# The mLSTM over x in two chunks of 256 tokens with a second state between them, in place of one chunk of 512

## The chip, the cores and the metric

The kernel runs on one core of a Trainium2 chip. Its time is the device time of one execution in microseconds. TensorE (PE, with its weight loads as PEld), VectorE (DVE), ScalarE (ACT), GpSimd (POOL) and the queues of SyncE (SP) that issue DMAs each work through a list of instructions of their own in order, and wait for one another by semaphores. Matmul operands and results of the vector engines lie in SBUF, matmul results in PSUM.

## The reference

Two layers run over 512 tokens `x` and 256 context tokens `ctx`. In each, the tokens are normalised and projected (`w_in`), go through three mixers side by side (an mLSTM of 4 heads of 128, a Fourier mix, a convolution of 31 taps), are projected back (`w_out`) and go through an MLP of 4096. The second layer gives out x alone, so its context goes only through what the mLSTM needs of it. The mLSTM is a linear attention with gates, run forward and backward. The reference goes chunk by chunk (64 tokens) and carries a state `C`, `n`, `m`:

```python
def step(carry, inp):
    C, n, m = carry
    ...
    S = jnp.einsum('bhld,bhsd->bhls', qc, kc) * jnp.exp(D - m_t[..., None])
    num = w_inter[..., None] * jnp.einsum('bhed,bhld->bhle', C, qc) + jnp.einsum('bhls,bhse->bhle', S, vc)
    den = w_inter * jnp.einsum('bhd,bhld->bhl', n, qc) + jnp.sum(S, axis=-1)
    h = num / jnp.maximum(jnp.abs(den), jnp.exp(-m_t))[..., None]
    ...
    C_new = decay[..., None, None] * C + jnp.einsum('bhs,bhse,bhsd->bhed', ws, vc, kc)
    n_new = decay[..., None] * n + jnp.einsum('bhs,bhsd->bhd', ws, kc)
```

The context goes first and its last state is the first state of x, in both directions. The length of a chunk changes only the order of the sums: inside a chunk every pair of tokens is a score, across chunks the state stands for what came before.

## The kernel before

**Tiles.** All 768 tokens (256 of the context, 512 of x, in blocks of 128) stay in SBUF. The large products take each operand as a rounded part and a remainder (`hi`, `lo`; L219 and L220 make them for the weights, L230 and L233 for the activations) and three matmuls in place of one. Weights come by DMA in the order of `stream`, two pieces ahead (`prep`, L213).

**Order.** A tile framework lays out the program: it takes the instructions in the order of the code, with priorities, and fixes for each engine the list in which they run. The taps of the convolution (L679, DVE) have a lower priority, so they fill DVE's gaps. A pool of tiles hands its buffers out in the order of the code: `t4` has 8 buffers of 4 KB per partition, `c2` 5 of 2 KB, `aux` and `mm` 4 PSUM banks each. `tc.cur_priority` and the pools are all that sets the order here.

**The mixer of a layer.** The chunks of `w_in` are taken in the order `CHUNKS`: t, a, t, a, then q, k, o for each of the four heads, then the Fourier chunk. `stationary` (L463) is the product of one chunk: 24 weights by 512 tokens of x, with the context 24 more by 256. After the o chunk of head h the generator `mlstm(h)` is staged, and each later chunk advances it by a step, so the work of a head lies between the products of the next head's chunks. Its three steps, for x:

- step 1: the split of q and k (L230, L233), the broadcast of the row of maxima `mb` by DMA (L814), for the state of the context two transposes of k (L818), their four weightings `kw` on ACT (L822) and four matmuls (L842, 129 columns: 128 of v and one of ones) into `cp`, copied to `cs` (L844). `qs` is q times the weight of the state (L825 on ACT, L826 on DVE). For each of the four key blocks j of x the scores against all 512 queries (L793, three matmuls of 512 columns), the weights exp (L836, ACT) over the 512, 384, 256 or 128 queries that each direction needs, the triangle of the diagonal block cut out on POOL (`masked`, L771), and the product of weights and scores (L838, DVE) into the tile `E`.
- step 2: for each query block and direction the sum in PSUM of the state's term and of one term for each key block (L862; 28 matmuls of 129 columns for x), then the quotient and the moments on DVE (`head_out`, L748 to L760).
- step 3: the transposes back (L777) and the gate (`group_out`).

The context, in the first layer only, has a step 1 and 2 of its own with one chunk of 256 (L793, L804, L807), which the change does not alter in what it computes. On POOL's queue, beside the masks, stand the DMAs of the Fourier tables (L196), which wait for a weight buffer. `gate_columns` makes the small columns of weights (`pcol`, `em`, `wc`); the row of maxima goes through HBM (`md`, L637) and comes back as `m0` (L647).

Of the kernel before, what the change touches and what calls it, by code (L numbers as in the profile page):

```python
# [10 lines left out]
F32 = mybir.dt.float32  # L11
F32R = mybir.dt.float32r
AF = mybir.ActivationFunctionType
ALU = mybir.AluOpType
# [3 lines left out]
SEQ = 512  # L18
CTX = 256
TOK = CTX + SEQ  # L20
NB = TOK // 128
CB = CTX // 128
# [26 lines left out]
ZW = 2 * 1 + 1 + TOK  # L49
QW = ZW - 2  # L50
XQ = CTX + 1
PAD = 15

DEFER, TAPS, LATER, AHEAD, PER = 1, 7, 300, 2, 3
# [10 lines left out]
def build(tc, a):  # L65
# [6 lines left out]
    small = pool("small", 2)  # L72
# [13 lines left out]
    def nm(s):  # L86
        n_names[0] += 1
        return f"{s}{n_names[0]}"

    def t4(*dims):  # L90
        t = t4p.tile([128, 1024], F32, tag="t4", name=nm("t4_"))
        return t
# [4 lines left out]
    def c2():  # L97
        return c2p.tile([128, 512], F32, tag="c2", name=nm("c2_"))
# [4 lines left out]
    def aux():  # L103
        return aup.tile([128, 512], F32, tag="aux", name=nm("aux_"))
# [4 lines left out]
    V, S, P, T = nc.vector, nc.scalar, nc.gpsimd, nc.tensor  # L109
    dma = nc.sync.dma_start  # L110
# [31 lines left out]
    ident = cload("ident", [128, 128])  # L142
# [8 lines left out]
    md = [drp.tile([8, TOK], F32, name=f"md{l}") for l in range(DEPTH)]  # L151
# [322 lines left out]
    def layer(l, res, nbg, first=None):  # L474
# [22 lines left out]
        vt = [t3()[:, :NB * 129].rearrange("p (b n) -> p b n", b=NB) for _ in range(H)]  # L497
# [111 lines left out]
        for q in range(2):  # L609
            ps = aux()  # L610
            for i in range(3):
# [3 lines left out]
                         bias=cols[64:128, C_BG:C_BG + 1])  # L615
# [24 lines left out]
        pcol = small.tile([128, NB, 2, 4], F32, tag="pcol", name=nm("pcol"))  # L640
        em = small.tile([128, NB, 2, 4], F32, tag="em", name=nm("em"))
        wc = small.tile([128, CB, 2, 4], F32, tag="wc", name=nm("wc"))
        mdv = md[l][:].rearrange("(d h) t -> h d t", d=2)

        m0 = small.tile([128, 2, 4], F32, tag="m0", name=nm("m0"))
        for d, t0 in ((0, CTX - 1), (1, 0)):
            dma(m0[:, d, :], md[l][4 * d:4 * d + 4, t0].partition_broadcast(128))  # L647

        def gate_columns():
            for q in range(2):  # L650
                ps = aux()
                for i in range(3):
                    T.transpose(ps[:, 128 * i:128 * i + 128], pm[:, 128 * (3 * q + i):128 * (3 * q + i) + 128], ident)
                v4 = ps[:, :384].rearrange("p (b g d n) -> p b g d n", b=3, g=2, d=2)
                for i in range(3):
                    V.tensor_copy(pcol[:, 3 * q + i], v4[:, i, 0, :, 0:4])
                    S.activation(em[:, 3 * q + i], v4[:, i, 1, :, 0:4], AF.Exp, scale=-1.0)
            for j in range(CB):
                V.tensor_tensor(wc[:, j], pcol[:, j], m0, ALU.subtract)
            S.activation(wc, wc, AF.Exp)  # L660

        y = {}

# [59 lines left out]
        def short_conv(outs, w, ranges):  # L723
# [12 lines left out]
            if i0 == 0:  # L736
                P.memset(q[:, CTX:XQ], 0.0)
            for k in (0, 2):
                V.scalar_tensor_tensor(q[:, i0:QW], zq[:, i0 + k:QW + k], w(k), q[:, i0:QW], ALU.mult, ALU.add)
            return q  # L740

        def kcol(j):
            return 128 * j if j < CB else XQ + 128 * (j - CB)

        def head_out(ps, b, h, hn, ba):
            den = ps[:, 128:258:129]
            d = ty(2, "d")
# [21 lines left out]

        def masked(E, fwd):  # L770
            P.affine_select(E, E, pattern=[[1 if fwd else -1, 128]], compare_op=ALU.is_ge, fill=0.0, base=0,  # L771
                            channel_multiplier=-1 if fwd else 1)
# [10 lines left out]
        def mlstm(h, q, k, to):  # L783
            y[h] = t3()
            groups = []
            qh, ql, kh, kl = [t3(F32R) for _ in range(4)]
            i0 = XQ if last else 0
            for src, hi, lo in ((q, qh, ql), (k, kh, kl)):
                split(src[:, i0:QW], hi[:, i0:QW], lo[:, i0:QW], True)

            def scores(out, kc, q0, n):
                for i, (kp_, qp) in enumerate(((kh, qh), (kh, ql), (kl, qh))):
                    T.matmul(out, kp_[:, kc:kc + 128], qp[:, q0:q0 + n], start=i == 0, stop=i == 2)  # L793

            if not last:
                mb = c2().rearrange("p (d t) -> p d t", d=2)
                dma(mb, mdv[h, :, 0:CTX].partition_broadcast(128))
                qk = aux()
                E = t4().rearrange("p (j d t) -> p j d t", j=2, d=2)
                for j in range(2):  # L800
                    scores(qk[:, 256 * j:256 * j + 256], 128 * j, 0, CTX)
                for j, d in ((0, 0), (0, 1), (1, 0), (1, 1)):
                    lo, hi = (128 * j, CTX) if d == 0 else (0, 128 * j + 128)
                    S.activation(E[:, j, d, lo:hi], mb[:, d, lo:hi], AF.Exp, scale=-1.0,  # L804
                                 bias=pcol[:, j, d, h:h + 1])
                    masked(E[:, j, d, 128 * j:128 * j + 128], d == 0)
                    V.tensor_tensor(E[:, j, d, lo:hi], E[:, j, d, lo:hi], qk[:, 256 * j + lo:256 * j + hi], ALU.mult)  # L807

                def c_terms(b, d, E=E):
                    js = range(0, b + 1) if d == 0 else range(b, CB)  # L810
                    return [(E[:, j, d, 128 * b:128 * b + 128], vt[h][:, j, :]) for j in js]
                groups.append((0, range(CB), c_terms))
            mb = t4().rearrange("p (d t) -> p d t", d=2)
            dma(mb, mdv[h, :, CTX:TOK].partition_broadcast(128))  # L814

            kp = aux()
            for j in range(CB):
                T.transpose(kp[:, 128 * j:128 * j + 128], k[:, 128 * j:128 * j + 128], ident)  # L818
            kw = c2().rearrange("p (d j n) -> p d j n", d=2, j=CB)
            for d in range(2):  # L820
                for j in range(CB):
                    S.activation(kw[:, d, j, :], kp[:, 128 * j:128 * j + 128], AF.Copy, scale=wc[:, j, d, h:h + 1])  # L822
            qs = t4().rearrange("p (d t) -> p d t", d=2)
            for d in range(2):
                S.activation(qs[:, d, :], mb[:, d, :], AF.Exp, scale=-1.0, bias=m0[:, d, h:h + 1])  # L825
            V.tensor_tensor(qs, qs, q[:, XQ:XQ + SEQ].unsqueeze(1).to_broadcast([128, 2, SEQ]), ALU.mult)  # L826
            Es = {}
            for j in range(CB, NB):
                qk = aux()
                scores(qk, kcol(j), XQ, SEQ)  # L830
                E = t4().rearrange("p (d t) -> p d t", d=2)
                Es[j] = E
                s0 = 128 * (j - CB)
                for d in range(2):
                    lo, hi = (s0, SEQ) if d == 0 else (0, s0 + 128)
                    S.activation(E[:, d, lo:hi], mb[:, d, lo:hi], AF.Exp, scale=-1.0, bias=pcol[:, j, d, h:h + 1])  # L836
                    masked(E[:, d, s0:s0 + 128], d == 0)
                    V.tensor_tensor(E[:, d, lo:hi], E[:, d, lo:hi], qk[:, lo:hi], ALU.mult)  # L838
            cp = aux()
            for d in range(2):  # L840
                for j in range(CB):
                    T.matmul(cp[:, 129 * d:129 * d + 129], kw[:, d, j, :], vt[h][:, j, :], start=j == 0, stop=j == CB - 1)  # L842
            cs = c2()[:, :258]
            S.activation(cs, cp[:, :258], AF.Copy)  # L844

            def x_terms(b, d):
                s0 = 128 * (b - CB)
                js = range(CB, b + 1) if d == 0 else range(b, NB)
                return [(qs[:, d, s0:s0 + 128], cs[:, 129 * d:129 * d + 129])] + \
                       [(Es[j][:, d, s0:s0 + 128], vt[h][:, j, :]) for j in js]  # L850
            groups.append((CTX, range(CB, NB), x_terms))
            yield
            hns = []
            for t0, bs, terms in groups:
                hn = c2()
                ba = tiny.tile([128, 4, 2], F32, tag="ba", name=nm("ba"))
                for i, b in enumerate(bs):
                    ps = aux()
                    for d in range(2):
                        ts = terms(b, d)  # L860
                        for n, (st_, mv) in enumerate(ts):
                            T.matmul(ps[:, 129 * d:129 * d + 129], st_, mv, start=n == 0, stop=n == len(ts) - 1)  # L862
                    head_out(ps, b, h, hn[:, 128 * i:128 * i + 128], ba[:, i])
                r = rsd(ba, len(bs))
                for i in range(len(bs)):
                    hb = hn[:, 128 * i:128 * i + 128]
                    V.tensor_scalar(hb, hb, ba[:, i, 0:1], r[:, i:i + 1], ALU.subtract, ALU.mult)
                hns.append((hn, 128 * len(bs), t0))
            yield
            for hn, n, t0 in hns:  # L870
                group_out(hn, n, t0, h, to)
# [583 lines left out]
```

## Time and profile before

| | |
|---|---|
| median of 3 runs | 1532.19 us (1530.03 to 1533.87) |
| profiled execution, its own time | 1534.91 us |
| its span | 1532.9 us |
| TensorE busy | 1488.5 us, 97% |
| DVE, ACT, POOL busy | 1101.4, 754.9, 94.0 us |
| granted TensorE clock | 0.998 |

Busy time is a sum over the span. TensorE's busy share says that it is rarely idle, not how fast it is; a stretch of the timeline tells how far apart its matmuls start. The mixer of the first layer with its mLSTM lies at about 140 to 340 us, that of the second at 960 to 1140. The trace records an fp32 matmul (L842, L862) twice and a transpose or an fp32r matmul (L818, L793) once.

### The profile page before, as it was taken

What the parts mean: (1) busy time and instruction counts of PE and PEld (TensorE: products, weight loads), DVE (VectorE), ACT (ScalarE), POOL (GpSimd) and SP (SyncE); (2) the same over time, 40 slices, a digit from 0 to 9 for tenths busy, and PEclk for the clock granted to TensorE, in tenths of its full rate; (3) what the DMA queues carried; (4) which work ended last, traced back from release to release, by engine and by line L of the source; (5) the groups of instructions that cost most, each with busy time, mean ns of one, the idle gap of its engine ahead of it and who ended that gap; (6) DMA issues with size and microseconds to landing.
All of it is one profiled execution on the core that took longest, in us unless ns stands there. A gap on an engine that the chain in (4) does not pass through costs nothing. (4 is left out here: it accounts for less than half of the span.)

```text
span 1532.9 us, 23301 instructions
## 1 busy us (share of the span) xinstructions
PE 1488.5 (97%) x8926; PEld 1303.6 (85%) x8926; DVE 1101.4 (72%) x2129; ACT 754.9 (49%) x1471; POOL 94.0 (6%) x233
## 2 busy tenths in 40 slices
PE   7999999999999999999999999999999999999998
PEld 4878888887888898898988979877888889999887
DVE  3359997754899886666865575898756886677666
ACT  4634245535745352442534576544437665555544
POOL 0002012200100000000000010111101000000000
PEclk9999999999999999999999999999999999999999
DMA  8445435523532452442622343422224133332224
GB/s 330 140 159 186 158 125 194 199 83 117 186 124 92 146 189 76 158 132 88 193 86 80 99 171 105 129 78 78 88 71 166 66 111 110 111 109 91 83 94 148
DMA packets 66015, 197.30 MB, mean 129 GB/s; under 512 B 11952, under 2 KB 14416, under 8 KB 65904
## 3 DMA queue, kind: packets, MB, share of 16 engines
q1 hardware_dynamic: 64464, 191.10, 37.5%
q0 software_dynamic: 1440, 4.72, 1.0%
q8 instruction: 70, 1.15, 0.3%
q14 instruction: 41, 0.34, 0.1%
HBM read 183.13 MB, written 12.66 MB: 128 GB/s over the span
## 5 line engine op out<-in xcount | busy, mean ns | idle before, releaser
L219 ACT ACTIVATE hi<-raw 128x1024 fp32r<-128x1024 f32 (+1 forms) x245 | 244.1, 999 | 397.0 <-PE mm L1052 134.9
L1052 PE MATMUL mm<-hi,t 128*128 128x512 f32 (+1 forms) x1296 | 406.1, 391 | 0.0
L220 DVE TENSOR_TENSOR lo<-raw,hi 128x1024 fp32r<-128x1024 f32 (+1 forms) x245 | 280.7, 1148 | 75.4 <-ACT hi L219 37.6
L1052 PEld LDWEIGHTS mm<-hi,t 128*128 128x128 f32 x1296 | 242.4, 188 | 54.7 <-DVE t L1220 0.4
L1052 PE MATMUL mm<-lo,t 128*128 128x512 f32 (+1 forms) x648 | 253.7, 391 | 0.0
L463 PE MATMUL mm<-hhi,hi 128*128 128x256 f32 (+1 forms) x576 | 168.3, 336 | 0.0
L463 PE MATMUL mm<-hlo,hi 128*128 128x256 f32 (+1 forms) x576 | 166.0, 332 | 0.0
L463 PE MATMUL mm<-hhi,lo 128*128 128x256 f32 (+1 forms) x576 | 165.0, 331 | 0.0
L1052 PEld LDWEIGHTS mm<-lo,t 128*128 128x128 f32 x648 | 121.8, 188 | 26.0
L1121 PE MATMUL mm<-hhi,hi 128*128 128x384 f32 (+1 forms) x448 | 139.5, 311 | 3.0 <-ACT c L1147 1.8
L1121 PE MATMUL mm<-hhi,lo 128*128 128x384 f32 (+1 forms) x448 | 138.5, 309 | 1.5 <-DVE lo L220 1.5
L1220 DVE TENSOR_TENSOR t<-mm,t 128x512 f32<-128x512 f32 x120 | 81.8, 688 | 79.5 <-PE mm L1052 79.4
L1121 PE MATMUL mm<-hlo,hi 128*128 128x384 f32 (+1 forms) x448 | 138.4, 309 | 0.0
L463 PEld LDWEIGHTS mm<-hhi,hi 128*128 128x128 f32 x576 | 107.1, 188 | 15.0 <-issue 2.5
L463 PEld LDWEIGHTS mm<-hhi,lo 128*128 128x128 f32 x576 | 108.3, 188 | 11.0
L463 PEld LDWEIGHTS mm<-hlo,hi 128*128 128x128 f32 x576 | 108.0, 188 | 11.0 <-issue 0.4
L679 DVE SCALAR_TENSOR_TENSOR t<-t,half,t 128x783 f32<-128x783 f32 (+1 forms) x120 | 102.3, 889 | 0.4
L1121 PE MATMUL mm<-t,hi 128*128 128x384 f32 (+1 forms) x448 | 97.4, 308 | 0.0
L1121 PEld LDWEIGHTS mm<-hhi,hi 128*128 128x128 f32 x448 | 84.4, 188 | 6.8 <-ACT c L1147 3.0
L1121 PEld LDWEIGHTS mm<-hhi,lo 128*128 128x128 f32 x448 | 84.3, 188 | 1.9 <-DVE lo L220 1.9
L1121 PEld LDWEIGHTS mm<-hlo,hi 128*128 128x128 f32 x448 | 84.4, 188 | 1.2
L233 DVE TENSOR_TENSOR t<-c,t 128x256 fp32r<-128x256 f32 (+1 forms) x132 | 62.2, 478 | 31.9 <-ACT t L230 31.5
(245 smaller groups left out, 2732.2 us busy)
## 6 DMA issues: line engine op xcount, KB each, us to landing
raw<-w SPq DMA_DIRECT2D x128, 512.0 KB, 4.3
raw<-w_at SPq DMA_DIRECT2D x48, 512.0 KB, 3.6
raw<-w_a SPq DMA_DIRECT2D x44, 512.0 KB, 4.3
raw<-w_c SPq DMA_DIRECT2D x32, 512.0 KB, 3.5
xd<-t SPq DMA_DIRECT2D x20, 512.0 KB, 2.9
raw<-w_o SPq DMA_DIRECT2D x16, 512.0 KB, 6.0
t<-xd SPq DMA_DIRECT2D x20, 256.0 KB, 6.0
t<-x SPq DMA_DIRECT2D x8, 512.0 KB, 6.0
```

What stands on the lines that cost most here:

```text
L219: S.activation(hi[:, r0:n0], raw[:, r0:n0], AF.Copy)
L220: V.tensor_tensor(lo[:, r0:n0], raw[:, r0:n0], hi[:, r0:n0].bitcast(F32), ALU.subtract)
L233: V.tensor_tensor(blk_lo, src, blk_hi.bitcast(F32), ALU.subtract)
L463: T.matmul(o[:, :n], wp[:, k, :], hp[:, k, t0:t0 + n], start=k == 0 and i == 0, stop=k == KB - 1 and i == 2)
L679: V.scalar_tensor_tensor(o, u[j][:, o0 + k:o1 + k], w, o, ALU.mult, ALU.add)
L1052: T.matmul(ps, hp[:, 128 * b:128 * b + 128], wp[:, f % 2, c0:c1], start=f == fs[0] and at[0] == 0 and n == 0, stop=f == fs[-1] and at[1] = ...
L1121: T.matmul(ps[:, :HN], wp[:, K2 * j + k, :], hp, start=first and k == 0 and i == 0, stop=k == K2 - 1 and i == 2, skip_group_check=True)
L1220: V.tensor_tensor(ac_, ps, ac_, ALU.add)
```

## The change

x is taken in two chunks of 256 (`CH`). Scores and weights are made inside a chunk alone (`weighted`, which the context now uses as well), so each chunk has two key blocks by 256 queries. Between the chunks stands a second state `cs1` for each direction: k of the chunk that comes first in that direction is transposed (L841: four transposes) and weighted (`kx`, L843, four on ACT), multiplied with v (L862, four matmuls), and the first state, decayed by `dec`, is added on DVE (L866). The second chunk's queries take `cs1` in place of `cs`. The exponent of `qs` is now four activations of 256 columns. `m1`, the maxima at the border, comes by two more small DMAs; `wx` and `dec` are made in `gate_columns`. `kw` and `kx` now lie in one tile of `t4`, where `kw` had one of `c2`.

```diff
+            for i in range(4):
+                V.tensor_tensor(wx[:, i], pcol[:, CB + i, i // 2], m1[:, i // 2], ALU.subtract)
+            S.activation(wx, wx, AF.Exp)
+            V.tensor_tensor(dec, m0, m1, ALU.subtract)
+            S.activation(dec, dec, AF.Exp)
...
+            def weighted(mb, kc, q0, blk):
+
+                qk = aux()
+                E = t4().rearrange("p (j d t) -> p j d t", j=2, d=2)
+                for j in range(2):
+                    scores(qk[:, CH * j:CH * j + CH], kc + 128 * j, q0, CH)
+                for j, d in ((0, 0), (0, 1), (1, 0), (1, 1)):
+                    lo, hi = (128 * j, CH) if d == 0 else (0, 128 * j + 128)
+                    S.activation(E[:, j, d, lo:hi], mb[:, d, lo:hi], AF.Exp, scale=-1.0,
+                                 bias=pcol[:, blk + j, d, h:h + 1])
+                    masked(E[:, j, d, 128 * j:128 * j + 128], d == 0)
+                    V.tensor_tensor(E[:, j, d, lo:hi], E[:, j, d, lo:hi], qk[:, CH * j + lo:CH * j + hi], ALU.mult)
+                return E
...
+            kt = t4()
+            kw = kt[:, 0:512].rearrange("p (d j n) -> p d j n", d=2, j=CB)
+            kx = kt[:, 512:1024].rearrange("p (i n) -> p i n", i=4)
...
-            kw = c2().rearrange("p (d j n) -> p d j n", d=2, j=CB)
...
+            kp = aux()
+            for i in range(4):
+                T.transpose(kp[:, 128 * i:128 * i + 128], k[:, XQ + 128 * i:XQ + 128 * i + 128], ident)
+            for i in range(4):
+                S.activation(kx[:, i, :], kp[:, 128 * i:128 * i + 128], AF.Copy, scale=wx[:, i, h:h + 1])
             qs = t4().rearrange("p (d t) -> p d t", d=2)
             for d in range(2):
-                S.activation(qs[:, d, :], mb[:, d, :], AF.Exp, scale=-1.0, bias=m0[:, d, h:h + 1])
+                for c in range(2):
+                    m_ = m0 if c == d else m1
+                    S.activation(qs[:, d, CH * c:CH * c + CH], mb[:, d, CH * c:CH * c + CH], AF.Exp, scale=-1.0,
+                                 bias=m_[:, d, h:h + 1])
...
-            for j in range(CB, NB):
-                qk = aux()
-                scores(qk, kcol(j), XQ, SEQ)
-                E = t4().rearrange("p (d t) -> p d t", d=2)
...
+            Ex = [weighted(mb[:, :, CH * c:CH * c + CH], XQ + CH * c, XQ + CH * c, CB + 2 * c) for c in range(2)]
...
+            cp = aux()
+            for d in range(2):
+                for j in range(2):
+                    i = 2 * d + j
+                    T.matmul(cp[:, 129 * d:129 * d + 129], kx[:, i, :], vt[h][:, CB + i, :], start=j == 0, stop=j == 1)
+            cs1 = c2()[:, :258]
+            for d in range(2):
+                dd = slice(129 * d, 129 * d + 129)
+                V.scalar_tensor_tensor(cs1[:, dd], cs[:, dd], dec[:, d, h:h + 1], cp[:, dd], ALU.mult, ALU.add)
...
-                js = range(CB, b + 1) if d == 0 else range(b, NB)
-                return [(qs[:, d, s0:s0 + 128], cs[:, 129 * d:129 * d + 129])] + \
-                       [(Es[j][:, d, s0:s0 + 128], vt[h][:, j, :]) for j in js]
+                c = (b - CB) // 2
+                return [(qs[:, d, s0:s0 + 128], (cs if c == d else cs1)[:, 129 * d:129 * d + 129])] + \
+                    within(Ex[c], b, CB + 2 * c, d)
```

On TensorE, step 1 of the second layer's first head stands before as follows (`t_1617` and `t_1619` are the split q and k, `aux` the PSUM banks, `c_1623` is `kw`; of the twelve scores the first of two banks and the last of all are shown):

```order
L818 MATMUL aux_9736<-ident_sb,t_1606_9641 128x128 x2
L793 MATMUL aux_9748<-t_1617_9726,t_1619_9728 128x512
...
L793 MATMUL aux_9759<-t_1617_9726,t_1619_9728 128x512
...
L793 MATMUL aux_9781<-t_1617_9726,t_1620_9729 128x512
L842 MATMUL aux_9792<-t_1516_8895,c_1623_9739 128x129 x4
L463 MATMUL mm_9821<-hhi,hi_9654 128x256
```

With the change the same place reads (lines are those of the changed kernel; `t_1624` holds `kw` and `kx`; of the twelve scores the first and the last):

```order
L835 MATMUL aux_9789<-ident_sb,t_1608_9693 128x128 x2
L841 MATMUL aux_9796<-ident_sb,t_1608_9693 128x128 x4
L801 MATMUL aux_9811<-t_1619_9778,t_1621_9780 128x256
...
L801 MATMUL aux_9831<-t_1619_9778,t_1622_9781 128x256
L855 MATMUL aux_9851<-t_1515_8935,t_1624_9788 128x129 x4
L862 MATMUL aux_9858<-t_1515_8935,t_1624_9788 128x129 x4
L464 MATMUL mm_9888<-hhi,hi_9706 128x256
```

Four banks of scores became two, four transposes and four matmuls of the second state were added, and the state's bank comes third and fourth after the two banks of the transposes.

On ACT, in the second layer, the weights of the second head (tile `t_1679` is its `mb`) stand before in this order, the last of its eight ahead of its own `kw` (L822):

```order
L825 ACTIVATE t_1682_10069<-t_1679_10059,m_9359 128x512 x2
L836 ACTIVATE t_1684_10077<-t_1679_10059,pcol_9356 128x512
L836 ACTIVATE t_1684_10077<-t_1679_10059,pcol_9356 128x128
...
L836 ACTIVATE t_1686_10088<-t_1679_10059,pcol_9356 128x384
...
L836 ACTIVATE t_1690_10110<-t_1679_10059,pcol_9356 128x512
...
L822 ACTIVATE c_1681_10064<-aux_10061,wc_9358 128x128 x4
```

With the change (`t_1680` is `mb`, `t_1681` holds `kw` and `kx`) the second head's work on ACT is one row of instructions:

```order
L838 ACTIVATE t_1681_10120<-aux_10121,wc_9398 128x128 x4
L843 ACTIVATE t_1681_10120<-aux_10128,wx_9402 128x128 x4
L848 ACTIVATE t_1684_10137<-t_1680_10118,m_9399 128x256
...
L811 ACTIVATE t_1686_10144<-t_1680_10118,pcol_9396 128x256
...
L811 ACTIVATE t_1688_10164<-t_1680_10118,pcol_9396 128x256
L857 ACTIVATE c_1690_10188<-aux_10183 128x258
```

The weights of the state and all the exponents of x moved behind the transposes of the same head's k.

## Rows read from the trace of the kernel before

**Rows 1.** The page, part 1: busy us (share of the span), instructions
```profile
PE 1488.5 (97%) x8926; PEld 1303.6 (85%) x8926; DVE 1101.4 (72%) x2129; ACT 754.9 (49%) x1471; POOL 94.0 (6%) x233
```

**Rows 2.** Busy us by stretch: length, PE, PEld, DVE, ACT, POOL, clock, DMA share, GB/s
```profile
140.00:240.00 100.00, 99.06 (x695) 81.47 (x697) 90.91 (x198) 33.53 (x65) 11.57 (x33) 1.00 0.43 144
240.00:340.00 100.00, 97.68 (x649) 87.38 (x650) 71.25 (x209) 49.23 (x104) 19.68 (x44) 1.00 0.52 172
960.00:1060.00 100.00, 95.61 (x505) 79.83 (x505) 91.33 (x159) 48.52 (x89) 12.33 (x37) 1.00 0.29 93
1060.00:1140.00 80.00, 78.29 (x487) 68.58 (x486) 59.45 (x172) 34.45 (x67) 12.35 (x29) 1.00 0.27 88
```

**Rows 3.** Waits of TensorE, 140 to 340: us in total, times, longest
```profile
PE aux L777 <- DVE c L867: 2.6, 2, 1.7
```

**Rows 4.** Waits of TensorE, 960 to 1140
```profile
PE aux L777 <- DVE c L867: 2.3, 2, 1.4
PE aux L793 <- DVE t L233: 1.6, 2, 0.8
PE aux L842 <- DVE t L838: 1.3, 1, 1.3
```

**Rows 5.** Timeline of TensorE: start us, us, engine, line, form, count
```profile
159.77 0.87 PE L793 MATMUL aux<-t,t 128*128 128x256 f32 x6
160.48 0.38 PE L818 MATMUL aux<-ident_sb,t 128*128 128x128 f32 x2
...
1086.02 3.11 PE L793 MATMUL aux<-t,t 128*128 128x512 f32 x12
1088.97 1.05 PE L842 MATMUL aux<-t,c 128*128 128x129 f32 x8
...
1118.71 0.38 PE L862 MATMUL aux<-c,t 128*128 128x129 f32 x2
...
1124.73 0.39 PE L862 MATMUL aux<-t,t 128*128 128x129 f32 x2
1124.88 0.48 PE L903 MATMUL aux<-hi,t 128*128 128x512 f32 x1
...
1190.96 1.09 PE L423 MATMUL aux<-ident_sb,t 128*128 128x128 f32 x8 [0.64 <-ACT t L410]
```

**Rows 6.** Groups by line and form: busy us, mean ns | idle before
```profile
L771 POOL TENSOR_SCALAR_AFFINE_SELECT t<-t 128x128 f32<-128x128 f32 x80 | 41.3, 537 | 226.3 <-ACT t L836 147.5 <-ACT em L657 67.5 <-ACT t L804 10.2
...
L753 DVE SCALAR_TENSOR_TENSOR c<-aux,rd,c 128x128 f32<-128x128 f32 x40 | 13.8, 345 | 0.0
...
L838 DVE TENSOR_TENSOR t<-t,aux 128x256 f32<-128x256 f32 x16 | 6.0, 414 | 0.0
...
L838 DVE TENSOR_TENSOR t<-t,aux 128x128 f32<-128x128 f32 x16 | 4.5, 280 | 0.0
```

**Rows 7.** Timeline of ScalarE, second layer's first head
```profile
990.42 2.50 ACT L836 ACTIVATE t<-t,pcol 128x128 f32<-128x128 f32 x6
...
1009.28 1.13 ACT L822 ACTIVATE c<-aux,wc 128x128 f32<-128x128 f32 x4
```

**Rows 8.** Timeline of VectorE, the products of that head
```profile
1014.02 3.27 DVE L838 TENSOR_TENSOR t<-t,aux 128x512 f32<-128x512 f32 x8
```

**Rows 9.** The chain, 1005 to 1025: start us, us, what
```profile
1014.02 0.89 DVE t L838 x2
...
1014.95 1.16 PE aux L842 x8
1016.11 8.32 PE mm L463 x48
```

**Rows 10.** Waits of all engines
```profile
POOL lo L196 <- PE mm L463: 15.1, 2, 11.2
```

**Rows 11.** Timeline of the SyncE queue
```profile
978.99 0.97 SPq L647 DMA_DIRECT2D m<-md  x2
```

More of the change, by code (lines that the diff above doesn't have):

```diff
@@ L51 @@
 XQ = CTX + 1
+CH = 256
 PAD = 15
@@ L645, in layer @@
         m0 = small.tile([128, 2, 4], F32, tag="m0", name=nm("m0"))
-        for d, t0 in ((0, CTX - 1), (1, 0)):
+        m1 = small.tile([128, 2, 4], F32, tag="m1", name=nm("m1"))
+        dec = small.tile([128, 2, 4], F32, tag="dec", name=nm("dec"))
+        wx = small.tile([128, 4, 4], F32, tag="wx", name=nm("wx"))
+        for d, t0, t1 in ((0, CTX - 1, CTX + CH - 1), (1, 0, CTX + CH)):
             dma(m0[:, d, :], md[l][4 * d:4 * d + 4, t0].partition_broadcast(128))
+            dma(m1[:, d, :], md[l][4 * d:4 * d + 4, t1].partition_broadcast(128))
         def gate_columns():
@@ L740, in short_conv @@
             return q
-        def kcol(j):
-            return 128 * j if j < CB else XQ + 128 * (j - CB)
         def head_out(ps, b, h, hn, ba):
@@ L793, in scores, with within @@
                     T.matmul(out, kp_[:, kc:kc + 128], qp[:, q0:q0 + n], start=i == 0, stop=i == 2)
+            def weighted(mb, kc, q0, blk):
[10 more added lines that the diff above has]
+                return E
+            def within(E, b, blk, d):
+                i = b - blk
+                js = range(0, i + 1) if d == 0 else range(i, 2)
+                return [(E[:, j, d, 128 * i:128 * i + 128], vt[h][:, blk + j, :]) for j in js]
             if not last:
@@ L797, in mlstm @@
                 dma(mb, mdv[h, :, 0:CTX].partition_broadcast(128))
-                qk = aux()
[L799 to L812, printed above, removed]
+                Ec = weighted(mb, 0, 0, 0)
+                groups.append((0, range(CB), lambda b, d: within(Ec, b, 0, d)))
             mb = t4().rearrange("p (d t) -> p d t", d=2)
             dma(mb, mdv[h, :, CTX:TOK].partition_broadcast(128))
+            kt = t4()
+            kw = kt[:, 0:512].rearrange("p (d j n) -> p d j n", d=2, j=CB)
+            kx = kt[:, 512:1024].rearrange("p (i n) -> p i n", i=4)
             kp = aux()
@@ L822, in mlstm @@
                     S.activation(kw[:, d, j, :], kp[:, 128 * j:128 * j + 128], AF.Copy, scale=wc[:, j, d, h:h + 1])
+            kp = aux()
[3 more added lines that the diff above has]
+                S.activation(kx[:, i, :], kp[:, 128 * i:128 * i + 128], AF.Copy, scale=wx[:, i, h:h + 1])
             qs = t4().rearrange("p (d t) -> p d t", d=2)
             for d in range(2):
-                S.activation(qs[:, d, :], mb[:, d, :], AF.Exp, scale=-1.0, bias=m0[:, d, h:h + 1])
+                for c in range(2):
+                    m_ = m0 if c == d else m1
+                    S.activation(qs[:, d, CH * c:CH * c + CH], mb[:, d, CH * c:CH * c + CH], AF.Exp, scale=-1.0,
+                                 bias=m_[:, d, h:h + 1])
             V.tensor_tensor(qs, qs, q[:, XQ:XQ + SEQ].unsqueeze(1).to_broadcast([128, 2, SEQ]), ALU.mult)
-            Es = {}
-            for j in range(CB, NB):
-                qk = aux()
-                scores(qk, kcol(j), XQ, SEQ)
-                E = t4().rearrange("p (d t) -> p d t", d=2)
[L832 to L838, printed above, removed]
+            Ex = [weighted(mb[:, :, CH * c:CH * c + CH], XQ + CH * c, XQ + CH * c, CB + 2 * c) for c in range(2)]
             cp = aux()
```

## The prediction

> **What bounds the kernel now.** I read the page's part 1 first: TensorE is busy for 97% of the span [rows 1], so a change in its work shows in the time wherever nothing else is late. Then the stretches in which the mixers lie: in the first layer TensorE is idle for 0.9 and 2.3 us of 100, in the second for 4.4 of 100 and 1.7 of 80 [rows 2], 9.4 us in all. DVE stands at 91% where TensorE is idle most (960 to 1060), ACT never above 49%. So in both mixers TensorE sets the pace, and in the second layer DVE is close behind it. The waits of TensorE say the same: each of those listed ends on DVE [rows 3, 4]. Only two touch what is changed: the splits of q and k come late for the scores (1.6 us), and the state's matmuls L842 wait once for a product of DVE that frees a PSUM bank (1.3 us), in the second layer's first head. There the chain goes from the products on DVE to the state, and then on TensorE alone [rows 9]. The DMA share is 0.27 to 0.52 and is no bound.
>
> A duration of one matmul overlaps the next one, so I price TensorE by the distance from one start to the next in the timeline [rows 5]. Scores of 512 columns: twelve between 1086.02 and 1088.97, 0.246 us each. Scores of 256 columns (the context's): six between 159.77 and 160.48, 0.118 each. Terms of 129 columns: 28 between 1118.71 and 1124.88, 0.220 each (the row counts two records for one). Transposes: eight in 1.09, 0.136 each with the end of the last in it.
>
> **The change part by part, per head.**
> - Scores: still twelve matmuls for x, of 256 columns in place of 512: 12 x (0.246 - 0.118) = 1.54 us less.
> - Terms: in place of ten key blocks a direction there are six (1 + 2 in each chunk), and the state's four stay. 28 become 20: 8 x 0.220 = 1.76 less.
> - Second state: four transposes at 0.136, 0.54 more, and four matmuls of 129 columns at 0.220, 0.88 more. The row of four of them alone gives 1.05 us [rows 5], the upper end; for a transpose the row of two (0.38) gives 0.19 each, the score of 256 columns 0.118: 0.3 us a head either way for the two together.
> - Sum on TensorE: 1.88 less a head, 15.0 for the eight heads, with 2.4 us up and down from the bounds. All of it is on TensorE's list, between products that wait for nothing, so it counts unless TensorE then waits.
>
> The count of matmuls does not change, which is why the widths matter. The Trainium skill speaks against the first term here: "TensorE: Matmul & The Clock Gate", section "Back-to-back issue gap", gives a sustained spacing of 81 ns at 128 columns and 131 ns at 512, since the weight load is paid with each matmul. On a line between these, an estimate from that page, 256 columns would cost 98 ns, the scores would gain 3.2 us in all and not 12.3, and the sum would be 5.9. The rows at 512 and 256 columns stand 2.1 to 1 and leave no fixed part, so the trace disagrees with it, and I go by the trace.
>
> - DVE: eight products (3.27 us in one row, [rows 8]) become four of 256 and four of 128 columns, 4 x 0.414 + 4 x 0.280 = 2.78; two additions for the second state have no row, the nearest is L753, 128 columns from PSUM with a scalar, 0.345 each [rows 6], bounds 0.2 and 0.5. So DVE's work stays within 0.5 us a head, up or down. It gets no lighter while TensorE does. The five small operations of the gates fall in the second layer in DVE's full stretch, under 1 us a layer; I take nothing, since TensorE has its products of q and k there.
> - ACT: four weightings more (1.13 us, [rows 7]), four activations of 256 in place of two of 512, eight exponents that get shorter. About 1 us more a head on an engine half empty: nothing.
> - Order of ACT: before, the exponents of x wait only for the row of maxima, and those of the second head stand ahead of its own weightings. Now `kt` is taken from the same pool first, and the tiles of `qs` and the exponents come after it, so on ACT all of it is one row behind the transposes of the same k: 1.13 + 1.13 us of weightings, four and eight exponents at no more than 0.42 (six in 2.50, [rows 7]), 5.0, and the copy of the state behind them, 0.4: 7.7 us from the transposes, and a mask and a product more (0.54 and 0.41, [rows 6]), 8.6 us to the last term. What covers it is TensorE's own list: scores 1.4, two states 1.8, and the products of the next chunk. In the second layer's first head these are 48, 8.32 us [rows 9], 11.5 in all: covered. For its third and fourth head the program puts fewer products in between and other work of ACT into the row, so there the cover is about as long as the row. DVE, which is in order too, stands with its eight products behind that row and loses what ACT's pace (0.42) exceeds its own (0.35), about 1 us a head with the masks. I take 1 us of new waits on TensorE for each head of the second layer, where DVE is full, and 0.25 in the first: 5 us. Bounds: nothing, if TensorE's list covers all, and the row less its scores and states for every head of the second layer, 4 x 5.4 = 22 us, if the products came first; it is nearer to the lower one since 48 products cover most heads.
> - The wait of 1.3 us [rows 4] goes: the state's bank is now that of the transposes, which ACT frees early. The splits (1.6) stay late.
> - Two small DMAs a layer: two took 0.97 us to issue on SP [rows 11], and the row of maxima is queued behind them, as are the weights. The exponents are needed 20 us later: hidden. Uncovered it would be 1 us a layer.
>
> Sum: -15.0 - 1.3 + 5 = -11.3 us. The profiled execution took 1534.9, 2.7 above the median, and would take 1523.6; against the median of 1532.2 that is 1520.9.
>
> **The rivals.**
> 1. DVE bounds the second layer's mixer. For: 91% in 100 us and no lighter work. Then only the first layer gains, 7.5 less 1.0 us of waits: 6.5, 1525.7. Against: TensorE is still busier there than DVE, and from 1060 on DVE has 25% to spare.
> 2. The new waits don't come, and all of the work goes with the old wait: -16.3, 1515.9. For: the cover of 11.5 against 8.6 us. Against: ACT's row is longer in two heads.
> 3. Slower. On POOL the masks stand in one queue with the DMAs of the Fourier tables, which wait for a weight buffer that TensorE frees, 11.2 us in the longest case [rows 10]. Before, most masks of x were done long ahead; now they are needed within a few us. If in each layer one head's masks stand behind such a wait, that is 2 x 11.2 - 15.0 = 7.4 us slower, 1539.6. It decides from 7.5 us a layer that the products in between don't cover, and these are 8.3 us long, so that I hold it for unlikely.
> 4. Nothing to measure: on top of the forecast's waits, one head in each layer waits out ACT's row, 2 x 5.4 us: -11.3 + 10.8, 1531.7. For: two heads whose cover is about as long as the row. Against: in the first layer DVE and ACT have room.
>
> **How the numbers follow.** A difference under 0.3% (4.6 us) can't be told from none. The forecast 1520.9 (1518 to 1524) has 0.54, rival 2 has 0.15, rival 1 has 0.17, rival 4 0.08, rival 3 0.06. Faster is the first three, 0.86; same 0.08; slower 0.06. The range reaches from just past rival 2 to just short of rival 4, 1515 to 1531, and leaves out the slower case and the tails.
>
> **What would show it.** The profile after should have rows of twelve scores at 0.118 us and 20 terms in 4.4 us in each head; TensorE's busy time in the two mixers less by about 15 us; L842's wait on DVE gone; new waits of the terms (L862 before) on ACT, DVE or POOL of about 5 us, most of them in the second layer. TensorE idle by over 10 us more in the second mixer would make the forecast wrong, as would masks that wait on POOL behind a table, or scores of 256 columns that start more than 0.16 us apart.

## The result, and the profile after

The changed kernel took 1514.92 us in the median of four runs (1513.57 to 1516.26); the kernel before took 1532.74 beside it (1530.03 to 1533.87). The ratio is 0.9886, with a 95% interval of 0.9869 to 0.9903: 17.8 us less, where 11.3 were forecast. That lies at the lower edge of the range of 1515 to 1531 (0.1 us under 1515), below the forecast's own range (1518 to 1524), and 1 us under the time of rival 2 (1515.9). The profiled execution took 1513.57 with a span of 1511.9.

Part 1 of the page of the changed kernel, to be read beside [rows 1]:
```profile
PE 1471.7 (97%) x8894; PEld 1292.6 (85%) x8894; DVE 1093.8 (72%) x2155; ACT 757.9 (50%) x1523; POOL 84.4 (6%) x233
```
TensorE is busy for 16.8 us less and still for 97% of the span: nearly all that it lost came off the time. DVE is 7.6 us lighter.

Busy time by stretch in the changed kernel, columns as in [rows 2]; the second layer's stretches start 10 us earlier, as the work does:
```profile
140.00:240.00 100.00, 98.80 (x712) 81.80 (x711) 91.29 (x207) 39.59 (x88) 11.42 (x32) 1.00 0.41 143
240.00:340.00 100.00, 97.79 (x644) 87.95 (x643) 69.63 (x212) 52.23 (x121) 17.81 (x44) 1.00 0.51 176
950.00:1050.00 100.00, 97.61 (x538) 83.08 (x537) 93.32 (x191) 48.38 (x102) 9.83 (x31) 1.00 0.28 90
1050.00:1130.00 80.00, 79.00 (x487) 69.37 (x486) 57.18 (x156) 40.14 (x88) 13.32 (x31) 1.00 0.29 101
```
TensorE's idle time is 1.2, 2.2, 2.4 and 1.0 us, 6.8 in all, where it was 9.4 before. It fell, although the new row on ACT was to make it grow by 5.

The waits of TensorE in the changed kernel, first from 140 to 345, then from 955 to 1150, beside [rows 3, 4]:
```profile
PE aux L785 <- DVE c L889: 3.2, 3, 1.2
PE aux L722 <- DVE d L756: 0.2, 1, 0.2
...
PE aux L785 <- DVE c L889: 1.9, 2, 1.7
PE aux L722 <- DVE c L715: 0.8, 1, 0.8
PE aux L801 <- DVE t L234: 0.7, 1, 0.7
PE aux L424 <- ACT t L411: 0.7, 1, 0.7
```
The states (L855, L862) wait for nothing, so the old wait of L842 is gone. The terms (L884) wait for nothing either: the new waits did not come. The scores' wait for the splits (L801 on L234) fell from 1.6 to 0.7.

TensorE's timeline in the second layer's first head (start us, us, then what), the place of the forecast's terms:
```profile
999.17 0.60 PE L841 MATMUL aux<-ident_sb,t 128*128 128x128 f32 x4
999.53 0.48 PE L801 MATMUL aux<-t,t 128*128 128x256 f32 x2
1000.73 1.47 PE L801 MATMUL aux<-t,t 128*128 128x256 f32 x10 [0.72 <-DVE t L234]
1002.04 1.06 PE L855 MATMUL aux<-t,t 128*128 128x129 f32 x8
1002.93 1.06 PE L862 MATMUL aux<-t,t 128*128 128x129 f32 x8
1003.74 0.60 PE L464 MATMUL mm<-hhi,hi 128*128 128x256 f32 x2
...
1012.16 0.38 PE L884 MATMUL aux<-c,t 128*128 128x129 f32 x2
...
1016.40 0.39 PE L884 MATMUL aux<-t,t 128*128 128x129 f32 x2
1016.54 0.48 PE L464 MATMUL mm<-hhi,hi 128*128 128x512 f32 x1
```
From one start to the next, as in [rows 5]: ten scores in 1.31 us, 0.131 each on average (0.22 from the first to the second, 0.12 from there on); four transposes in 0.36, 0.09 each; the second state in 0.81; the 20 terms in 4.38, 0.219 each.

ACT and DVE beside that (same columns): the row that was to be too long.
```profile
999.88 1.12 ACT L838 ACTIVATE t<-aux,wc 128x128 f32<-128x128 f32 x4
1000.88 1.16 ACT L843 ACTIVATE t<-aux,wx 128x128 f32<-128x128 f32 x4
1001.88 1.74 ACT L848 ACTIVATE t<-t,m 128x256 f32<-128x256 f32 x4
1003.48 2.90 ACT L811 ACTIVATE t<-t,pcol 128x256 f32<-128x256 f32 x8
1006.25 0.39 ACT L857 ACTIVATE c<-aux 128x258 f32<-128x258 f32 x1
```
```profile
1007.17 1.30 DVE L850 TENSOR_TENSOR t<-t,t 128x1024 f32<-128x1024 f32 x1
1008.40 2.19 DVE L814 TENSOR_TENSOR t<-t,aux 128x256 f32<-128x256 f32 x8
1010.52 0.59 DVE L866 SCALAR_TENSOR_TENSOR c<-c,dec,aux 128x129 f32<-128x129 f32 x2
```
ACT is done at 1006.64, 6.8 us after it began. DVE came to the products later than that, since it had taps and a split in front of them, and ended at 1011.11. The first term starts at 1012.16: 1.05 us were to spare. The same rows in the third and fourth head:
```profile
1076.58 0.41 ACT L857 ACTIVATE c<-aux 128x258 f32<-128x258 f32 x1
1077.36 0.38 PE L884 MATMUL aux<-c,t 128*128 128x129 f32 x2
1077.56 0.60 DVE L866 SCALAR_TENSOR_TENSOR c<-c,dec,aux 128x129 f32<-128x129 f32 x2
...
1099.31 0.60 DVE L866 SCALAR_TENSOR_TENSOR c<-c,dec,aux 128x129 f32<-128x129 f32 x2
1100.72 0.39 PE L884 MATMUL aux<-c,t 128*128 128x129 f32 x2
```
From the end of L866 to the first L884 there are 0.81 us in the fourth head and, in the second, 2.97. In the third the additions end behind the first term (1078.15 against 1077.36). That term takes the first state (in every head it does, by the code), whose copy L857 was done at 1077.00, 0.36 us before. So the cover was as thin as the forecast said, and it held.

### The profile page after: what moved, and what is told of

It is laid out like the page before. It is cut to its first block, busy times and chain, and to the rows that moved or that the text cites. A ratio compares the mean times of both kernels' runs of the same rounds, so it can differ in the third digit from the quotient of the medians.

```text
span 1511.9 us, 23296 instructions
## 1 busy us (share of the span) xinstructions
PE 1471.7 (97%) x8894; PEld 1292.6 (85%) x8894; DVE 1093.8 (72%) x2155; ACT 757.9 (50%) x1523; POOL 84.4 (6%) x233
## 5 line engine op out<-in xcount | busy, mean ns | idle before, releaser
L1074 PE MATMUL mm<-hi,t 128*128 128x512 f32 (+1 forms) x1296 | 406.4, 392 | 0.1
L1074 PEld LDWEIGHTS mm<-hi,t 128*128 128x128 f32 x1296 | 242.3, 188 | 54.9 <-DVE t L234 1.1
L1074 PE MATMUL mm<-lo,t 128*128 128x512 f32 (+1 forms) x648 | 253.4, 391 | 0.0
L464 PE MATMUL mm<-hhi,hi 128*128 128x256 f32 (+1 forms) x576 | 167.9, 336 | 0.0
L464 PE MATMUL mm<-hlo,hi 128*128 128x256 f32 (+1 forms) x576 | 165.8, 332 | 0.0
L464 PE MATMUL mm<-hhi,lo 128*128 128x256 f32 (+1 forms) x576 | 165.2, 331 | 0.0
L1074 PEld LDWEIGHTS mm<-lo,t 128*128 128x128 f32 x648 | 121.9, 188 | 26.3
L464 PEld LDWEIGHTS mm<-hhi,hi 128*128 128x128 f32 x576 | 106.7, 188 | 14.9 <-issue 2.9
L464 PEld LDWEIGHTS mm<-hhi,lo 128*128 128x128 f32 x576 | 108.2, 188 | 10.8
L464 PEld LDWEIGHTS mm<-hlo,hi 128*128 128x128 f32 x576 | 107.8, 188 | 11.3 <-issue 0.8
L234 DVE TENSOR_TENSOR t<-c,t 128x256 fp32r<-128x256 f32 (+1 forms) x132 | 62.1, 477 | 32.5 <-ACT t L231 31.7
```

Of the source, the lines that this page charges most:

```text
L234: V.tensor_tensor(blk_lo, src, blk_hi.bitcast(F32), ALU.subtract)
L464: T.matmul(o[:, :n], wp[:, k, :], hp[:, k, t0:t0 + n], start=k == 0 and i == 0, stop=k == KB - 1 and i == 2)
L1074: T.matmul(ps, hp[:, 128 * b:128 * b + 128], wp[:, f % 2, c0:c1], start=f == fs[0] and at[0] == 0 and n == 0, stop=f == fs[-1] and at[1] = ...
```

## The experiments

Each kernel was timed in several runs; ratios are to the kernel before on the same chip. As the traces also differ by up to 3.6 us in stretches that no edit touches (below), and the medians may with them, mixers are also read from the trace: from the first matmul of `stationary` (L464) to the first of the MLP's second product (L1074) in the first layer (M1), and from the last product of v to the same place in the second layer (M2). Before, M1 and M2 are 356.8 and 247.3 us; in the changed kernel 348.7 and 236.5, and when run again 349.8 and 237.3. So the mixers hold 18.9 us of the change, or 17.1 by the second trace, from which the mixers of the later kernels are counted. One thing holds for every edit below: the framework also lays the engines' lists out anew, so that a run shows the edit together with a changed order.

**The changed kernel again.**

> The changed kernel once more, as the reference for the runs beside it. 1514.9 us as before, within 2 us.

Measured: 1513.84 us, ratio 0.9869 (0.9851 to 0.9886). Once more, beside the last two kernels below:

> The changed kernel itself, beside the two below on the same chip: 1514.5 us, 1.5 up or down, by every theory.

Measured: 1514.42, ratio 0.9872 (0.9857 to 0.9886). The gain is steady at 18 to 20 us.

**Change in the first layer only, in the second layer only** (the old and the new code side by side under a test of `last`; the new gate columns and their small DMAs stay in both layers).

> The change in the first layer alone; the second layer takes x in one chunk of 512 as before. The landmarks of the two traces give 8.1 us of the gain to the first mixer and 10.8 to the second. Theory W, half of TensorE's work of 15 us: 7.5 to 8 us faster than before, 1525. Rival O, that a good part comes from the waits of the second layer: the first layer gives its 7.5 all the same, so the second alone (next run) tells; if the first gave 4 or less, the sum on TensorE would be wrong there.

> The change in the second layer alone. Theory W with work alone: 7.5 us faster, 1525.2. With the waits of the second layer that go as well (TensorE's idle time in its mixer is 6.1 us before and 3.4 after): 10 us faster, 1522.5. The prediction's rival 1, DVE as the bound of the second mixer: 0 to 2 us.

Measured: first layer 1523.70, ratio 0.9943 (0.9931 to 0.9955), 9.0 us less; second layer 1524.97, ratio 0.9946 (0.9934 to 0.9957), 7.7 less. Together 16.7, about the whole. By the landmarks M1 falls by 7.0 in the one and M2 by 10.4 in the other; the mixer that was left as before comes out 1.3 us shorter in the one and 2.0 longer in the other, which is about how far these landmarks can be trusted. The second layer's mixer gained as much as the first, with DVE at 93%: rival 1, by which DVE bounds it, falls.

**Scores of x twice.**
```diff
-                for j in range(2):
-                    scores(...)
+                for _ in range(2 if blk else 1):
+                    for j in range(2):
+                        scores(...)
```


> The changed kernel with each score matmul of x made twice, the second over the first: 12 more matmuls of 256 columns a head, 96 in all. Theory W, the time follows TensorE's own work: 96 x 0.118 us = 11.3 us more, 1526.2. Rival O, the gain came as much from the order and the waits, and TensorE has idle time there that takes the scores up: 0 to 5 us more, 1515 to 1520. A sentence of its own for the Trainium skill (TensorE: Matmul & The Clock Gate, Back-to-back issue gap): by an estimate from its 81 ns at 128 and 131 ns at 512 columns it would be 9.4 us.

Measured: 1531.62, ratio 0.9987 (0.9975 to 0.9998), 17.8 over the changed kernel. What is put on TensorE's list shows in the time, at no less than its own length: the price is above the eleven expected, not below. In the first mixer TensorE has these waits:
```profile
PE aux L801 <- DVE t L815: 4.2, 1, 4.2
PE aux L785 <- DVE c L890: 2.2, 3, 1.0
```
By the trace the longer scores hold their two banks longer, and once TensorE waits 4.2 us for a product of DVE to free one; from 260 to 270 us, right behind that wait, the granted clock is 0.85. With the 4.2 us the eleven come to 15.5; the mixers hold 14.4 (8.6 and 5.8), and the rest is within the drift.

**Second state left out** (all chunks take the first state).
```diff
-            cp = aux()
-            for d in range(2):
-                ...
-                    T.matmul(cp[...], kx[:, i, :], vt[h][:, CB + i, :], ...)
-            cs1 = c2()[:, :258]
-            ...
+            cs1 = cs
```


> The changed kernel without the second state: the four transposes of k, the four weightings, the four matmuls and the two additions of each head are left out, and the second chunk's queries take the first state. Theory W: 8 x (4 x 0.10 + 4 x 0.22) = 10.2 us less than the changed kernel, 1504.7 (at 0.136 a transpose 11.4 less). Rival O, that the second state's chain over ACT and DVE holds the heads back beside its matmuls: 14 us less or more, 1501 or below; if the state's work lies in TensorE's idle time: 0 to 4 less.

Measured: 1506.89, ratio 0.9822 (0.9805 to 0.9839), 6.95 less than the changed kernel; M1 and M2 fall by 4.0 and 6.3, 10.3 in all. That is the price of the second state on TensorE's list, and in the mixers it is what was expected; the median shows two thirds of it.

**Exponents of x twice.**
```diff
-                    S.activation(E[:, j, d, lo:hi], ...)
+                    for _ in range(2 if blk else 1):
+                        S.activation(E[:, j, d, lo:hi], ...)
```


> The changed kernel with each of the eight exponents of x made twice on ACT in every head: the row of ACT behind the transposes of k gets about 3 us longer (8 activations at 0.3 to 0.42 us). The prediction's step of new waits, with a cover as long as the row in the third and fourth head of the second layer and TensorE waiting 1 us a head there already: 2 x 3 us in these heads and some in the others, 6 to 12 us more, 1521 to 1527. The rival, that TensorE's own products cover the row with room to spare: 0 to 3 us more, 1515 to 1518.

Measured: 1525.59, ratio 0.9941 (0.9923 to 0.9959), 11.8 over the changed kernel, of which the mixers hold 6.3 (1.8 and 4.5). Now the terms wait. The waits of TensorE in the second mixer, and the row of the fourth head in its timeline:
```profile
PE aux L885 <- ACT c L858: 2.9, 1, 2.9
PE aux L885 <- DVE c L867: 1.1, 1, 1.1
...
1110.12 0.49 PE L885 MATMUL aux<-c,t 128*128 128x129 f32 x2 [2.85 <-ACT c L858]
```
A row on ACT that is longer by 2.8 us (5.67 in place of 2.90 for the exponents) is waited out in two heads of the second layer, the first and the fourth, and the row as it is in none. So the mechanism is there, but in the fourth head the cover became shorter as well. The Fourier products that TensorE has there between the states and the terms, in the changed kernel (L906) and here (L907):
```profile
1096.15:1100.70 4.55, 4.51 (x37) 4.50 (x37) 1.00 0.00 0
1104.70:1107.30 2.60, 2.52 (x19) 2.34 (x19) 1.00 0.00 0
```
In the new list 18 of them, 2.2 us by their starts, come behind the terms. With the old list the wait of 2.85 would have been about 0.7, an estimate from these rows.

**States behind the scores** (transposes, weightings and states after `qs` and the exponents in the code, so that ACT takes the exponents early as before the change).

> The changed kernel with the tile of kw and kx, the transposes and the weightings put behind the exponents and scores in the code, so that ACT can make the exponents of x ahead of the same head's transposes, as before the change. Theory W, that the row on ACT is covered: within 1.5 us of the changed kernel, 1514.9. The prediction's step of new waits, 1 us a head of the second layer and 0.25 in the first: 3 to 5 us faster than the changed kernel, 1510 to 1512.

Measured: 1521.24, ratio 0.9923 (0.9911 to 0.9935), some 7 us over the changed kernel. Neither theory had that. By the step in the forecast, the early exponents should have helped; the run loses 2.8 and 4.6 in the mixers. TensorE's timeline at the second layer's first head, DVE's, and the stretches around it:
```profile
1005.29 0.42 PE L801 MATMUL aux<-t,t 128*128 128x256 f32 x1 [1.95 <-DVE t L234]
1006.56 2.50 PE L801 MATMUL aux<-t,t 128*128 128x256 f32 x10 [0.85 <-DVE t L234]
```
```profile
993.32 1.21 DVE L836 TENSOR_TENSOR t<-t,t 128x1024 f32<-128x1024 f32 x1
...
1004.56 0.68 DVE L234 TENSOR_TENSOR t<-t,t 128x512 fp32r<-128x512 f32 x1
```
```profile
1000.00:1010.00 10.00, 7.14 (x32) 5.80 (x30) 10.00 (x17) 3.12 (x6) 0.00 (x0) 0.77 0.31 99
1010.00:1020.00 10.00, 10.00 (x59) 9.05 (x58) 8.49 (x17) 6.57 (x20) 3.63 (x6) 0.88 0.31 107
```
DVE multiplies q with its weights (L836) as soon as the exponents are there, ahead of the taps and splits that TensorE waits for next. The kernel before has this product in the same place (L826 at 997.06, the splits at 1009.02 and 1010.29) and waits 1.6 us there; in the changed kernel it comes behind the splits (L850 at 1007.17), and the wait is 0.7. Here TensorE idles 2.8 us, as six transposes, 0.6 us of its own work, have moved behind the scores as well. That is read from the traces and was not tried by itself. Then the granted clock is at the lower of its two levels, 1.2 GHz, for part of 20 us: the ten scores take 0.23 each in place of 0.131. With 0.77 and 0.88 granted, 4.6 + 2.4 = 7.0 us were at half the clock, which loses at most 3.5 us beside the waiting, as TensorE idled in part of them. The first mixer has such a place too, a wait of 1.73 us for the normalisation and the stretch around it:
```profile
196.23 0.30 PE L785 MATMUL aux<-ident_sb,c 128*128 128x128 f32 x1 [1.73 <-DVE c L889]
190.00:200.00 10.00, 8.27 (x45) 4.89 (x44) 8.23 (x17) 8.13 (x19) 3.05 (x12) 0.83 0.32 115
```

**Four chunks of 128 with three states between them.**

> x in four chunks of 128 with three states between them. A head has 12 scores of 128 columns, 16 terms (two for each block and direction), 4 + 6 matmuls of states and the same transposes. On TensorE against the changed kernel: scores 12 x (0.118 - 0.06 to 0.11) = 0.1 to 0.7 us less, terms 4 x 0.22 = 0.9 less, states 2 x 0.22 = 0.4 more: 0.6 to 1.1 less a head, 5 to 9 us in all, 1506 to 1510 by theory W. On DVE four more additions of 0.345 and 8 x 0.280 in place of 2.78 for the products, 0.8 us more a head; the rival, DVE as the bound of the second layer's mixer: the gain of the second layer turns into 3 us more, and the whole is 0 to 2 us faster or slower than the changed kernel.

Measured: 1520.92, ratio 0.9923 (0.9907 to 0.9938), 6 to 7 over the changed kernel where 5 to 9 less were expected. M1 is 350.1 and M2 240.5, neither less than with two chunks. TensorE's timeline in the first layer:
```profile
162.33 1.56 PE L802 MATMUL aux<-t,t 128*128 128x128 f32 x12
163.72 1.11 PE L867 MATMUL aux<-t,c 128*128 128x129 f32 x8
```
Twelve scores of 128 columns take 1.39 us, 0.116 each (0.16 for the first, 0.11 for the others), where those of 256 columns took 0.118 before the change [rows 5] and 0.131 in it (0.22 for the first, 0.12 for the others). Halving the width paid from 512 to 256 and gives next to nothing from 256 to 128. Where the fewer terms went is clear in part: states and terms wait for ACT 1.0 and 0.8 us in the two mixers, which they did not before, and after a wait of 2.56 us for the normalisation (L786) the granted clock is 0.83 from 1030 to 1040. The waits of L786 are 5.2 us in all, no more than the 5.1 of the changed kernel. Of the 6 to 7 us in the median the mixers hold 3.5.

**Normalisation on ACT, and the product of q on POOL.** The longest waits left go to DVE, so two kernels take work from it: in one L889 becomes an activation, in the other L850 is given to POOL.
```diff
-                    V.tensor_scalar(hb, hb, ba[:, i, 0:1], r[:, i:i + 1], ALU.subtract, ALU.mult)
+                    S.activation(hb, hb, AF.Identity, scale=r[:, i:i + 1], bias=nb[:, i:i + 1])
...
-            V.tensor_tensor(qs, qs, q[...], ALU.mult)
+            P.tensor_tensor(qs, qs, q[...], ALU.mult)
```


> The changed kernel, with the normalisation of each 128-token block of a head (L889) on ACT in place of DVE, and one small product on DVE for its bias. It is what the longest waits of TensorE that are left go back to (L785 on L889, 5.1 us in five waits). If those waits are DVE's load: 2 to 4 us less than the changed kernel, and the wait of L785 under 2.5 us. If they are the length of the row from the last term through moments and power to the transposes: no change, within 1.5 us, with L785 waiting on ACT in their place. If ACT's row of weights and exponents is the closer one now: slower by 1 to 4 us, with new waits of the terms L884 on ACT.

Measured: 1514.59, ratio 0.9875 (0.9855 to 0.9895): no difference from the changed kernel (0.9872). The wait in the second mixer only changed its name:
```profile
PE aux L785 <- ACT c L891: 2.1, 2, 1.8
```
So the wait doesn't come from this operation's place on DVE. It fits a row whose length counts, from the last term through moments, power and normalisation; whether DVE's load makes the earlier part of that row longer, this run doesn't tell.

> The changed kernel, with the product of q and its weights (L850, 128x1024, 1.30 us a head on DVE ahead of the eight products of the scores) on POOL in place of DVE. If TensorE's list sets the end and the row of ACT is covered: no change, within 1.5 us, although DVE has 10 us less. If DVE's load makes the waits that are left: 2 to 3 us less. If POOL is slow for it, the masks of x, which are queued behind it, come late and TensorE's terms L884 wait on DVE or POOL, most in the third and fourth head of the second layer where under 1 us was to spare: 3 to 8 us more.

Measured: 1525.99, ratio 0.9948 (0.9935 to 0.9961), 11.6 over the changed kernel, with M1 356.0 and M2 243.1. POOL's timeline in the second layer's first head, and what DVE waits for in that mixer:
```profile
1011.04 2.00 POOL L850 TENSOR_TENSOR t<-t,t 128x1024 f32<-128x1024 f32 x1 [32.90 <-ACT t L848]
1012.99 5.17 POOL L779 TENSOR_SCALAR_AFFINE_SELECT t<-t 128x128 f32<-128x128 f32 x8
```
```profile
DVE t L814 <- POOL t L779: 11.0, 3, 4.6
```
The third theory held, and the place was another: the terms wait for only 0.6 us, but DVE stands 11 us behind masks that are late, and all that DVE does next is late. TensorE's wait at L785 grows from 5.1 to 11.1 us over the run. It is 2.72 us at the longest in the first layer and 2.8 in the second, both with a lower clock behind them; the first:
```profile
199.84 0.49 PE L785 MATMUL aux<-ident_sb,c 128*128 128x128 f32 x2 [2.72 <-DVE c L889]
```
```profile
190.00:200.00 10.00, 7.28 (x46) 5.61 (x45) 5.64 (x13) 5.26 (x10) 2.57 (x13) 1.00 0.60 208
200.00:210.00 10.00, 10.00 (x51) 7.38 (x51) 8.48 (x12) 1.86 (x3) 0.00 (x0) 0.83 0.19 64
```
No experiment that computes everything beats the changed kernel.

## Why the prediction was right, and where it was off

- **TensorE bounds both mixers: right.** The idle time is 6.8 us of 380 after the change, the two layers gain separately and add up, and doubled scores cost at least their own length.
- **The work of 15.0 us: right within 1 us.** By the new rows a head gives 12 x (0.246 - 0.131) = 1.38 for the scores (forecast 1.54) and 1.75 for the terms (1.76), and costs 0.36 for the transposes (0.54) and 0.81 for the state (0.88): 1.96, 15.7 for eight heads. A lower gain of the scores and cheaper transposes, which are 0.09 and not 0.136, cancel. That is one head taken eight times; the starts of all these matmuls in both layers, less the waits in front of them, add up to 15.9 less than before.
- **The Trainium skill's spacing.** "TensorE: Matmul & The Clock Gate", section "Back-to-back issue gap", would by its sustained spacing have made the work 5.9 us, an estimate. The step from 512 to 256 columns went against it: 0.246 to 0.131. The step from 256 to 128 goes its way in kind, with a part that does not fall with the columns: 0.116 us. The page says 81 ns there.
- **The old wait of 1.3 us: right.** It is gone. The splits' wait, taken as staying at 1.6, fell to 0.7 (0.9 when run again).
- **New waits of 5 us: this is the step that failed.** "I take 1 us of new waits on TensorE for each head of the second layer" came out at none: the terms wait for nothing in either layer. The row was sized a little too long: ACT needed 6.8 us where 7.7 were reckoned, and eight products and two additions of DVE 2.71 where 3.5 were. A mask took 0.42 on average (L779, 80 in 30.6 us) where [rows 6] had 0.54, but 0.63 in the second layer's first head and 0.34 in its others. And the cover was not too short but just enough, with 1.05, 2.97, 0.36 and 0.81 us left by head. A margin of about 1 us, positive or nil, was priced as a wait of about 1 us. The doubled exponents show that the mechanism is there: with 2.8 us more, two heads wait, one of them with a shorter cover too.
- **The order on ACT.** The forecast saw it as a loss that the exponents no longer run ahead. The states put behind show no such gain: that run is some 7 us slower, in the second layer by the trace because DVE takes the product of q before the splits. As the transposes moved too, it doesn't price the exponents' place alone.
- **Rival 2 is what happened**, 1515.9 against 1514.9. Rival 1 falls by the second layer alone. Rival 3's mechanism, masks late on POOL, exists: with 2.0 us of other work ahead of them it costs 11.6 us. In the changed kernel TensorE waits for no mask and DVE 1.3 us for seven of them, although POOL stands up to 14.2 us behind a table's buffer (L197).

The sum as measured: 15.7 of work, 1.3 of the old wait, 0.9 of the splits, in all 17.9 us, against 17.8 in the medians. That these agree to 0.1 us is luck, as stretches without an edit differ by more. So TensorE's work was forecast rightly, and its price too; the time came out at the range's lower edge because 5 us of waits were added that did not come.

## What to carry to other kernels

Where an engine is busy for 97% and the others keep up, price a change by the distance between starts on that engine, measured at the new width, and a new dependence by the margin left at its consumer: margins of 0.4 to 3 us cost nothing here, and a row longer by 2.8 us cost 6.3 in the mixers. Moving work off a full engine gained nothing where only the last step of a row was moved, and lost where the work landed ahead of something in another in-order queue.

## What the runs showed of the hardware that was not expected

A gap on TensorE can cost more than itself. After gaps of 2.8 us (in two waits, states behind the scores), 2.85 (doubled exponents) and 2.72 us (product on POOL), the granted clock in the ten microseconds after was 0.88, 0.83 and 0.83, with matmuls twice as far apart in part of it; the same follows the gaps of 4.2 us (doubled scores, 0.85) and 2.56 us (chunks of 128, 0.83). The row of the doubled exponents is this:
```profile
1110.00:1120.00 10.00, 9.88 (x56) 9.20 (x57) 8.44 (x38) 6.07 (x13) 0.16 (x1) 0.83 0.28 111
```
In the changed kernel TensorE idles 1.67 us between 1020 and 1030, and the clock stays at its higher level:
```profile
1020.00:1030.00 10.00, 8.33 (x39) 6.46 (x38) 9.09 (x21) 2.50 (x4) 1.55 (x4) 1.00 0.17 54
```
The kernel with the normalisation on ACT idles 1.78 us in the same stretch, also at 1.00. Yet the stretch around the gap of 1.73 us in the first mixer of the states behind the scores has 0.83. So the length of the gap alone doesn't decide; what does was not tried. With 0.83 granted, 3.4 us of the ten were at the lower level, so such a gap costs some 1.7 us beyond itself.

Stretches that no edit touches differ by up to 3.6 us between these kernels: from the first product of the second MLP in layer 1 to the last of v in layer 2 they took 521.1 to 524.7 us, and the stretch after the second mixer 324.5 to 327.1. With the doubled exponents these two stretches hold 5.3 of the 5.5 us between the 11.8 of the median and the 6.3 of the mixers. It is also why a difference of 3 us between two kernels was not read as the edit's. Where this drift comes from stays open.
